# Eight weight tiles in a pool of their own at the upper end of SBUF

## The chip, the cores and the metric

The kernel runs on one core of one Trainium2 chip. The metric is the device time of one execution in microseconds (us); before the change the median of three runs is 2689.66 us, from 2688.57 to 2689.96. A core has TensorE (matmuls and transposes; PE in the profile, its loads of weights PEld), VectorE (DVE), ScalarE (ACT), GpSimd (POOL) and SyncE (SP), from whose queue this kernel issues its DMAs. SBUF is the memory on the core in which tiles lie; an address below is a byte offset in each of its 128 partitions. A matmul has a stationary operand, which a load of weights brings in, and a moving operand, which is read column by column.

## The reference

A trunk of two layers on 2048 rows of 1024 channels: a gated MLP with chunked spatial mixing, and band attention with a learned relative bias.

```python
# layer A
h = rms_norm(x, a_norm_g)
u, v, z = jnp.split(h @ w_in, 3, axis=-1)            # 1024 -> 3 x 2048
u = gelu(u); v = layer_norm(gelu(v), ln_g, ln_b)
mixed = einsum('hts,bgshc->bgthc', w_m, vg) + b_s    # 128-row chunks, masked
x = x + (u * mixed * silu(z)) @ w_out
# layer B
k, v = jnp.split(rms_norm(x, kv_norm_g) @ w_kv, 2, axis=-1)
q, z = jnp.split(rms_norm(x, b_norm_g) @ w_qz, 2, axis=-1)
sc = einsum('bqhd,bkhd->bhqk', q / 8, kc) + bias     # own and 8 earlier chunks of 64
o = einsum('bhqk,bkhd->bqhd', softmax(sc), vc)
x = x + (o * silu(z)) @ wb_out
return rms_norm(x, final_norm_g)
```

## The kernel before, in words

Each product in float32 is made as three matmuls in fp32r (`mm3`, lines 105 to 108): both operands are split into a high part, rounded by ScalarE, and a low part, which VectorE gets by subtracting the high part; the three matmuls add high times high, high times low and low times high. The lines 106, 107 and 108 of the profile are these three.

Layer A is done as block products in seven phases (`PH`, line 469) for each of six column groups of the input weights and for the output weights, after a scheme that needs seven products for eight blocks. A step is one phase of one pair of row blocks j: 12 matmuls for the input (`P` in the profile), 24 for the output (`Po`). The stationary operand is a tile of transposed activations, S, kept in DRAM and read again three steps ahead; the moving operand is T, the split combination of weight blocks that `make_t` (line 284) prepares: a DMA into a tile `raw` or `rw`, sums on GpSimd, then the high part by ScalarE (line 276) and the low part by VectorE (line 279). `in_t` (line 341) asks for the T tiles, two for each quarter of a phase, out of eight slots with the tag "T"; in the output projection the phases take turns between these slots and two large tiles, `hh` and `hl`, four quarters each (`in_big`, line 349).

Between the steps of layer A the gating stage runs: its mixing matmuls (`mx`, line 635) have the split mixing weights `ws` as stationary operand and the split normalized v, `vh` and `vl`, as moving operand; its results go to tiles `m`. These tiles lie in a pool `up` that is opened on the right side, from the upper end of SBUF downwards, and closed before the output projection. The pool `p0` of the first phases and the pool `po` of the output projection use the same end at other times.

Layer B normalizes and transposes 512 rows at a time (`norm_transpose`, line 128) into `hh` and `hl`, 16 KB per partition each. The projections (`one`, line 955, `pj` in the profile) have weights split by `load_split` (line 192) into two tiles of the tag "T" as stationary operand and `hh`, `hl` as moving operand; the projection of values (`vp`) has it the other way round; the output projection (`b4`, `bo`) moves weights of the tag "T" past the gated attention. Scores (`s`, line 1096), transposes of the probabilities (`tp`, line 1135) and their products with values (`pv`) are woven between the projections' matmuls by `take` (line 1314).

The pool `sh` (line 89) holds, from low to high addresses in the order of first use, four slots `raw` of 4 KB, the eight T slots of 4 KB, then `hh` and `hl`. Above it on the left side come the pools of layer A (`ca`, later `ug` and `poc`), and in layer B `cb` and `sb`.

Of the kernel before, what the change touches and what calls it, by code (L numbers as in the profile page):

```python
# [10 lines left out]
F32R = mybir.dt.float32r  # L11
# [6 lines left out]
P = 128  # L18
# [3 lines left out]
T = 512  # L22
# [11 lines left out]
def trunk_kernel(  # L34
# [52 lines left out]

    sm = ctx.enter_context(tc.tile_pool(name="sm", bufs=1))
    sh = ctx.enter_context(tc.tile_pool(name="sh", bufs=1))
    pmm = ctx.enter_context(tc.tile_pool(name="pmm", bufs=4, space=PSUM))  # L90

    class Late:
# [84 lines left out]
    def load_scaled(src, name, gain=None, keep=None):  # L177
        raw = sh.tile([P, 1024], F32, tag="raw", name=f"raw_{name}", bufs=4)
        nc.sync.dma_start(raw[:], src)
        if gain is not None:  # L180
            k = gain.shape[1]
            r3 = raw[:].rearrange("p (k c) -> p k c", k=k)
            nc.gpsimd.tensor_tensor(
                r3, r3, gain.broadcast_to([P, k, 1024 // k]), op=ALU.mult
            )
            if put_off:
                put_off[0](lambda: nc.sync.dma_start(keep, raw[:]))
            else:
                nc.sync.dma_start(keep, raw[:])
        return raw  # L190

    def load_split(*args):
        raw = load_scaled(*args)
        name = args[1]
        wh = sh.tile([P, 1024], F32R, tag="T", name=f"wh_{name}", bufs=8)
        wl = sh.tile([P, 1024], F32R, tag="T", name=f"wl_{name}", bufs=8)
        nc.scalar.copy(wh[:], raw[:])
        nc.vector.tensor_tensor(wl[:], raw[:], wh[:].bitcast(F32), op=ALU.subtract)
        return wh, wl
# [30 lines left out]
    with ExitStack() as actx:  # L230
# [110 lines left out]
        def in_t(n, ph):  # L341
            def where(q):
                return [
                    sh.tile([P, 1024], F32R, tag="T", name=f"T{n}_{ph}_{q}{i}", bufs=8)[:]
                    for i in range(2)
                ]
            return where
# [591 lines left out]
    with ExitStack() as bctx:  # L939
# [15 lines left out]
        def one(t, p, c):  # L955
            wh, wl = load_split(
                *kqz_source(t or p == 0, p, c)
            )
            acc = pmm.tile([P, T], F32, tag="mm", name=f"pj{t}_{p}_{c}")
            for k in range(KD):  # L960
                hh, hl = xT[t][k]
                sl = slice(k * P, (k + 1) * P)
                mm3(acc[:], wh[:, sl], wl[:, sl], hh, hl, k == 0, k == KD - 1)
                if k < KD - 1:
                    yield None
            yield acc

        def project(t, p, block=None):


            def proj_v(pp):
                w = []
                for half in range(2):
                    w.append(
                        load_split(
                            *v_source(t or pp == 0, pp, half)
                        )
                    )
# [216 lines left out]
        def b4(t, parts):  # L1195
# [5 lines left out]
            def prep(n):  # L1201
                if n == len(seq):
                    return
                dh, bl, k = seq[n]
                nm = f"{t}_{dh}_{bl[0]}_{k}"
                if k % 2 == 0:
                    wts[n] = wts[n + 1] = load_split(wb_out[dh, k // 2], f"bo{nm}")
                og = ogt[t, k]
                ts = slice(bl[0] * P, (bl[-1] + 1) * P)
                oh = sb.tile([P, len(bl) * P], F32R, tag="Q", name=f"oh{nm}", bufs=QB)  # L1210
                ol = sb.tile([P, len(bl) * P], F32R, tag="Q", name=f"ol{nm}", bufs=QB)
                nc.scalar.copy(oh[:], og[:, ts])
                nc.vector.tensor_tensor(ol[:], og[:, ts], oh[:].bitcast(F32), op=ALU.subtract)
                ogs[n] = (oh, ol)
# [210 lines left out]
```

## Time and profile before

| | before |
|---|---|
| median of 3 runs | 2689.66 us (2688.57 to 2689.96) |
| the profiled execution's own time | 2689.71 us |
| its span, first to last instruction | 2687.9 us |
| mean granted TensorE clock | 0.995 |
| bytes moved by DMA | 607.16 MB, 226 GB/s in the mean |

How to read it: the profile takes one execution. The span is the stretch from the first instruction to the last; the execution's own time has 1.8 us more around it. Groups of instructions are shown as line, engine, operation, written tile <- read tiles, shapes and count, then busy time in us and the mean of one in ns, then the idle time of the engine just before them and what ended it. Matmuls are pipelined: one lasts some 390 ns for 512 columns while the next starts 0.23 us after it. The view of one tile gives minimum, median and maximum instead of the mean.

The stages by time, from the profile's windows: TensorE is busy 288.65 of the first 300 us, 318.21 of the 320 us to 620, all of the 460 us to 1080, 269.84 of the 275 us to 1355 (the output projection of layer A and the end of what is before it), then 337.53 of 345, 647.40 of 650 and 323.95 of the last 338 us (attention).

### The profile page before, as it was taken

What the parts mean: (1) busy time and instruction counts of PE and PEld (TensorE: products, weight loads), DVE (VectorE), ACT (ScalarE), POOL (GpSimd) and SP (SyncE); (2) the same over time, 40 slices, a digit from 0 to 9 for tenths busy, and PEclk for the clock granted to TensorE, in tenths of its full rate; (3) what the DMA queues carried; (4) which work ended last, traced back from release to release, by engine and by line L of the source; (5) the groups of instructions that cost most, each with busy time, mean ns of one, the idle gap of its engine ahead of it and who ended that gap; (6) DMA issues with size and microseconds to landing.
All of it is one profiled execution on the core that took longest, in us unless ns stands there. A gap on an engine that the chain in (4) does not pass through costs nothing.

```text
span 2687.9 us, 39968 instructions
## 1 busy us (share of the span) xinstructions
PE 2645.6 (98%) x14176; PEld 2269.2 (84%) x14176; DVE 1933.5 (72%) x3187; ACT 1274.4 (47%) x2252; POOL 721.1 (27%) x775
## 2 busy tenths in 40 slices
PE   8999999999999999999999999999999999999997
PEld 7788888888888888788888888888988889888996
DVE  5655666766667667778666676877879777787777
ACT  5422242443434434323255554566655666556663
POOL 3511223141232413534034520211202111021110
PEclk9999999999999999999999999999999999999998
DMA  7899999986977868767576654544445454454331
GB/s 296 311 335 334 346 363 322 324 321 229 327 259 270 313 250 309 266 223 272 186 264 211 214 183 162 180 150 142 162 159 183 141 153 155 139 166 122 113 110 68
DMA packets 209190, 607.16 MB, mean 226 GB/s; under 512 B 24288, under 2 KB 24288, under 8 KB 208992
## 3 DMA queue, kind: packets, MB, share of 16 engines
q1 hardware_dynamic: 208992, 604.62, 65.4%
q8 instruction: 113, 1.85, 0.3%
q14 instruction: 85, 0.70, 0.1%
HBM read 466.11 MB, written 127.93 MB: 221 GB/s over the span
## 4 chain that ended last, share of the span: by engine, by line
PE 85%; DVE 5%; DMA 4%; POOL 2%; issue 2%; ACT 1%; SPq 0%; DVEq 0%; POOLq 0%; ACTq 0%
PE P L108 10%; PE P L107 10%; PE P L106 10%; PE pj L106 6%; PE pj L107 6%; PE pj L108 6%; PE s L1096 4%; PE tp L1135 4%; PE pv L1162 4%; PE Po L108 3%; PE Po L107 3%; PE Po L106 3%; PE vp L108 2%; PE vp L106 2%; PE vp L107 2%; PE bo L106 2%
## 5 line engine op out<-in xcount | busy, mean ns | idle before, releaser
L106 PE MATMUL P<-T,S 128*128 128x512 f32 x1248 | 495.1, 397 | 3.9 <-ACT S L276 2.1
L108 PE MATMUL P<-T,S 128*128 128x512 f32 x1248 | 489.4, 392 | 0.0
L107 PE MATMUL P<-T,S 128*128 128x512 f32 x1248 | 488.1, 391 | 1.1 <-DVE T L279 1.1
L1115 POOL TENSOR_SCALAR pr<-pr,sl 128x640 f32<-128x640 f32 (+4 forms) x256 | 202.0, 789 | 760.7 <-DVE sl L1114 662.2
L1111 ACT ACTIVATE pr<-pr,nm 128x640 f32<-128x640 f32 (+4 forms) x256 | 195.4, 763 | 266.2 <-DVE nm L1104 263.6
L106 PE MATMUL pj<-hh_b,wh_b 128*128 128x512 f32 x768 | 311.6, 406 | 0.2 <-ACT hh_b L166 0.2
L107 PE MATMUL pj<-hl_b,wh_b 128*128 128x512 f32 x768 | 302.6, 394 | 0.0
L108 PE MATMUL pj<-hh_b,wl_b 128*128 128x512 f32 x768 | 301.7, 393 | 0.0
L108 PEld LDWEIGHTS P<-T,S 128*128 128x128 f32 x1248 | 234.7, 188 | 50.1
L106 PEld LDWEIGHTS P<-T,S 128*128 128x128 f32 x1248 | 235.2, 188 | 49.4 <-ACT S L276 2.3
L107 PEld LDWEIGHTS P<-T,S 128*128 128x128 f32 x1248 | 235.2, 188 | 46.6 <-DVE T L279 1.3
L1139 DVE TENSOR_TENSOR pt<-tp,pt 128x640 fp32r<-128x640 f32 (+4 forms) x256 | 188.8, 738 | 59.7 <-ACT pt L1138 57.0
L1104 DVE CUSTOM_DVE_ANT_0 pr<-s,bias 128x640 f32<-128x640 f32 (+4 forms) x256 | 188.2, 735 | 46.7 <-PE s L1096 41.3
L108 PEld LDWEIGHTS pj<-hh_b,wl_b 128*128 128x128 f32 x768 | 144.4, 188 | 33.2
L1135 PE MATMUL tp<-ident,pr 128*128 128x128 f32 x1120 | 164.7, 273 | 6.2 <-DVE pt L1139 4.6
L1138 ACT CAST pt<-tp 128x640 fp32r<-128x640 f32 (+4 forms) x256 | 159.4, 623 | 22.6 <-PE tp L1135 18.0
L1135 PEld LDWEIGHTS tp<-ident,pr 128*128 128x128 f32 x1120 | 134.7, 140 | 33.6 <-POOL pt L1128 4.4
L106 PEld LDWEIGHTS pj<-hh_b,wh_b 128*128 128x128 f32 x768 | 144.8, 189 | 19.2 <-ACT hh_b L166 0.5
L107 PEld LDWEIGHTS pj<-hl_b,wh_b 128*128 128x128 f32 x768 | 145.2, 189 | 17.4
L106 PE MATMUL vp<-wh_bv,hh_b 128*128 128x256 f32 x512 | 148.5, 290 | 0.9 <-ACT hh_b L166 0.9
L108 PE MATMUL vp<-wh_bv,hl_b 128*128 128x256 f32 x512 | 145.6, 284 | 0.3
L107 PE MATMUL vp<-wl_bv,hh_b 128*128 128x256 f32 x512 | 145.2, 284 | 0.0
(220 smaller groups left out, 6052.4 us busy)
## 6 DMA issues: line engine op xcount, KB each, us to landing
S<-hsd SPq DMA_DIRECT2D x288, 512.0 KB, 5.0
rw<-in_w_a SPq DMA_DIRECT2D x108, 512.0 KB, 6.0
raw_b<-wk SPq DMA_DIRECT2D x75, 512.0 KB, 3.8
A<-ytd SPq DMA_DIRECT2D x72, 512.0 KB, 4.9
hsd<-S SPq DMA_DIRECT2D x56, 512.0 KB, 4.3
rwo<-in_w_out SPq DMA_DIRECT2D x40, 512.0 KB, 4.8
bias<-reld SPq DMA_DIRECT2D x64, 320.0 KB, 3.5
raw_bo<-in_wb_out SPq DMA_DIRECT2D x36, 512.0 KB, 3.9
```

The source lines that it names most:

```text
L106: mm(ps, lh, rh, start=first, stop=False)
L107: mm(ps, lh, rl, start=False, stop=False)
L108: mm(ps, ll, rh, start=False, stop=last)
L1096: mm(ps[:, sg, :w], q[:, qb * P : (qb + 1) * P], kx[:, koff + sg * w : koff + (sg + 1) * w], start=i == 0, stop=i == 1,)
L1104: nc.vector.tensor_tensor_reduce(out=pr[:, c0:].rearrange("p (a b) -> p a b", a=nseg), in0=ps[:, :nseg, :w], in1=bias[:, c0:].rearrange("p ...
L1111: nc.scalar.activation(pr[:, c0:], pr[:, c0:], AF.Exp, scale=-1.0, bias=nm[:], accum_out=sl[:])
L1115: nc.gpsimd.tensor_scalar(pr[:, c0:], pr[:, c0:], sl[:], 1.0, op0=ALU.mult, op1=ALU.mult)
L1135: tpose(tp[:, b, :], pr[:, b * P : (b + 1) * P], ident[:])
L1138: nc.scalar.copy(oh, tp[:, b0:5, :])
L1139: nc.vector.tensor_tensor(pt[:, 1, b0 + qq : 5 + qq, cs], tp[:, b0:5, :], oh.bitcast(F32), op=ALU.subtract)
L1162: mm(po[:, 0, :], keys(i), pt[:, j, i, :], start=(t == 0 and j == 0 and i == blocks[0]), stop=(j == 1 and i == blocks[-1]),)
```

## The change

The eight slots of the tag "T" move from the pool `sh` into a new pool `shT` that is opened right behind it with `side="right"`, so that it lies at the upper end of SBUF. Later pools on that side (`p0`, `up`, `po`) lie below it. The two tiles `hh` and `hl` of the transposed norm, which lay above T, take T's former place, and the left side's later pools start 32 KB lower.

```diff
@@ -87,6 +87,7 @@
     sm = ctx.enter_context(tc.tile_pool(name="sm", bufs=1))
     sh = ctx.enter_context(tc.tile_pool(name="sh", bufs=1))
+    shT = ctx.enter_context(tc.tile_pool(name="shT", bufs=1, side="right"))
     pmm = ctx.enter_context(tc.tile_pool(name="pmm", bufs=4, space=PSUM))
@@ -192,8 +193,8 @@
     def load_split(*args):
         raw = load_scaled(*args)
         name = args[1]
-        wh = sh.tile([P, 1024], F32R, tag="T", name=f"wh_{name}", bufs=8)
-        wl = sh.tile([P, 1024], F32R, tag="T", name=f"wl_{name}", bufs=8)
+        wh = shT.tile([P, 1024], F32R, tag="T", name=f"wh_{name}", bufs=8)
+        wl = shT.tile([P, 1024], F32R, tag="T", name=f"wl_{name}", bufs=8)
         nc.scalar.copy(wh[:], raw[:])
@@ -341,7 +342,7 @@
     def in_t(n, ph):
             def where(q):
                 return [
-                    sh.tile([P, 1024], F32R, tag="T", name=f"T{n}_{ph}_{q}{i}", bufs=8)[:]
+                    shT.tile([P, 1024], F32R, tag="T", name=f"T{n}_{ph}_{q}{i}", bufs=8)[:]
                     for i in range(2)
                 ]
             return where
```

The addresses in the two built programs, in bytes of a partition:

| tiles | before | after |
|---|---|---|
| `raw` (4 x 4096) | 4736 to 21120 | 4736 to 21120 |
| T (8 x 4096) | 21120 to 53888 | 196576 to 229344 |
| `hh`, `hl` (2 x 16384) | 53888 to 86656 | 21120 to 53888 |
| S (6 x 4096) | 137856 to 162432 | 105088 to 129664 |
| `ws` (2 x 4096) | 192480 to 200672 | 159712 to 167904 |
| `vh`, `vl` (3 x 4096) | 200672 to 212960 | 167904 to 180192 |
| `m` (4 x 4096) | 212960 to 229344 | 180192 to 196576 |

On no engine does an instruction change its place: the rows of the two programs stand in the same order on TensorE, VectorE, ScalarE, GpSimd and SyncE, with the same waits, so no rows are set against each other here. Below the new line 90 all line numbers are one higher.

## The prediction

> **What bounds the kernel now.** I read the page first: busy times, then the chain that ended last.
>
> ```profile
> span 2687.9 us, 39968 instructions
> ...
> PE 2645.6 (98%) x14176; PEld 2269.2 (84%) x14176; DVE 1933.5 (72%) x3187; ACT 1274.4 (47%) x2252; POOL 721.1 (27%) x775
> ...
> PE 85%; DVE 5%; DMA 4%; POOL 2%; issue 2%; ACT 1%; SPq 0%; DVEq 0%; POOLq 0%; ACTq 0%
> ```
>
> TensorE is busy for 2645.6 of 2687.9 us, so all that can be won or lost without touching its own pace is 42.3 us of idle time, and most of that is the start. So the time is 14176 matmuls times their pace, and a change matters here if it alters that pace or adds waits on TensorE. The execution profiled took 2689.71 us (span plus 1.8 us around it), 0.05 us over the median of 2689.66; the sum below is made against 2689.71. A measurement of this kernel tells about 0.2%, 5.4 us, from no change.
>
> Next, what TensorE waits for (microseconds in total, times, longest one):
>
> ```profile
> PE tp L1135 <- DVE pt L1139: 4.6, 3, 4.0
> ...
> PE P L107 <- DVE T L279: 1.1, 1, 1.1
> ...
> PE vp L106 <- ACT hh_b L166: 0.9, 3, 0.4
> ```
>
> The longest sum is 4.6 us. Waits for the writers of the tiles that the change moves are 1.1 us (T) and 0.9 us (hh): 2.0 us in the whole run. Their writers work far ahead.
>
> **The change part by part.** *Instructions.* None is added, removed or reordered: on all five engines the rows stand in the same order with the same waits, and each tile takes the same slot of its tag. What differs is addresses, in bytes of a partition. The eight T tiles go from 21120–53888 to 196576–229344. hh and hl go from 53888–86656 to 21120–53888, T's old place. Every other tile above them moves down by exactly 32768 and keeps its distance to its neighbours; raw stays. So the direct term is 0 instructions, 0 DMAs, 0 waits. What is left is whether an instruction takes longer or shorter because of where its operand lies.
>
> *T read by TensorE as the moving operand.* These are the dearest groups, with pj, where T is stationary and hh and hl move. Columns: count, busy us, mean ns.
>
> ```profile
> L106 PE MATMUL P<-T,S 128*128 128x512 f32 x1248 | 495.1, 397 | 3.9 <-ACT S L276 2.1 <-DMA S<-hsd 1.7
> L108 PE MATMUL P<-T,S 128*128 128x512 f32 x1248 | 489.4, 392 | 0.0
> L107 PE MATMUL P<-T,S 128*128 128x512 f32 x1248 | 488.1, 391 | 1.1 <-DVE T L279 1.1
> L106 PE MATMUL pj<-hh_b,wh_b 128*128 128x512 f32 x768 | 311.6, 406 | 0.2 <-ACT hh_b L166 0.2
> L107 PE MATMUL pj<-hl_b,wh_b 128*128 128x512 f32 x768 | 302.6, 394 | 0.0
> L108 PE MATMUL pj<-hh_b,wl_b 128*128 128x512 f32 x768 | 301.7, 393 | 0.0
> ...
> L106 PE MATMUL bo<-wh_bo,oh 128*128 128x512 f32 x256 | 101.2, 396 | 3.1 <-ACT oh L1212 3.1
> ...
> L106 PE MATMUL Po<-To,So 128*128 128x512 f32 x256 | 100.3, 392 | 0.0
> ```
>
> The means differ, 391 to 406 ns for the same shape, which could be the place of the operands. To see whether it is, take one stretch, 1120 to 1335 us, where the output projection reads its moving operand by turns from T and from hh and hl:
>
> ```profile
> L106 PE MATMUL Po<-To,So 128*128 128x512 f32 x166 | 64.6, 389 | 0.0
> L107 PE MATMUL Po<-To,So 128*128 128x512 f32 x166 | 64.6, 389 | 0.0
> ...
> L106 PE MATMUL Po<-To_hh,So 128*128 128x512 f32 x151 | 58.8, 389 | 0.0
> ...
> L107 PE MATMUL Po<-To_hl,So 128*128 128x512 f32 x151 | 58.7, 389 | 0.0
> ```
>
> 389 ns from all three regions. And the pj group itself, in a stretch where nothing of another shape stands between its matmuls (1358.5 to 1365.3 us), with the same hh, hl and T slots side by side:
>
> ```profile
> L107 PE MATMUL pj<-hl_b,wh_b 128*128 128x512 f32 x11 | 4.3, 390 | 0.0
> L108 PE MATMUL pj<-hh_b,wl_b 128*128 128x512 f32 x11 | 4.3, 390 | 0.0
> L106 PE MATMUL pj<-hh_b,wh_b 128*128 128x512 f32 x10 | 3.9, 389 | 0.0
> ```
>
> 389 to 390, not 406. The surplus therefore comes with the position in the stream (transposes and scores between the projection's matmuls), which is unchanged, and not with the place of hh, hl or T. hh and hl move into the very bytes that T is read from at 389 ns. Term: 0.
>
> *The upper end.* Before, the eight slots of 4 KB at 196576 to 229344 held exactly the second ws tile, the three vh and vl tiles and the four m tiles of the gating stage. TensorE read the first two kinds there, and ScalarE and VectorE wrote them. The gating matmuls mx answer for the reads (min/median/max ns), beside the nearest row at a low address, vp, which moves 256 columns of T (its mean follows its busy time):
>
> ```profile
> L106 PE MATMUL mx<-vh,ws x128: 280/282/283, 362.0 to 968.9; 128*128 128x256 f32 x128
> ```
>
> ```profile
> L107 PE MATMUL vp<-wl_bv,hh_b 128*128 128x256 f32 x512 | 145.2, 284 | 0.0
> ```
>
> 282 against 284 ns: nothing is lost at the upper end. It also answers for alignment: the slots of T started on a multiple of 64 bytes and now start 32 bytes past one, as vh, vl and ws did. Where T is the stationary operand, in pj, the load of weights is what reads it; loads from S and from the upper end (ws) stand against each other, in mean ns:
>
> ```profile
> L108 PEld LDWEIGHTS P<-T,S 128*128 128x128 f32 x1248 | 234.7, 188 | 50.1
> ...
> L108 PEld LDWEIGHTS mx<-vh,ws 128*128 128x128 f32 x128 | 24.1, 189 | 0.0
> ```
>
> What no row of before shows is a run of 512 moving columns that starts 32 bytes off. The bounds from the nearest rows: mx less vp, −2 ns, at the lower end; at the upper end pj's mean, (406 + 394 + 393) / 3 = 398, less 389, +9 ns. I take 0, since mx reads off that boundary twice in each matmul and shows no cost.
>
> *T written by ScalarE and VectorE.* Low address, then the same operations at the upper end:
>
> ```profile
> L276 ACT CAST T<-rw x42: 1028/1052/1085, 9.1 to 943.0; 128x1024 fp32r<-128x1024 f32 x42
> L279 DVE TENSOR_TENSOR T<-rw,T x42: 1209/1222/2311, 11.6 to 949.3; 128x1024 fp32r<-128x1024 f32 x42
> ```
>
> ```profile
> L276 ACT CAST vh<-va x32: 1036/1052/1057, 354.1 to 950.8; 128x1024 fp32r<-128x1024 f32 x32
> L279 DVE TENSOR_TENSOR vl<-va,vh x32: 1208/1225/2178, 355.2 to 959.7; 128x1024 fp32r<-128x1024 f32 x32
> ```
>
> Medians 1052 and 1052, 1222 and 1225: +3 ns on a subtraction. The loops make 258 such pairs (42 from rw as shown, 36 from the chain tiles, 16 for the output, 164 for the attention's weights), so 0.8 us of VectorE in 1933.5, behind TensorE's work. If that cover were gone, 0.8 us is the whole price. Term: 0.
>
> *Transfers.* No DMA writes T. Those into tiles that moved by 32768 are the same transfers to the same offsets; the commonest:
>
> ```profile
> S<-hsd SPq DMA_DIRECT2D x288, 512.0 KB, 5.0
> ```
>
> An S tile is asked for three steps ahead; a step is 12 matmuls, and the stretch of 215 us above has 950 of them, 0.226 us each, so 8.1 us ahead for a landing of 5.0. A change of 1 us in landing would stay hidden. Term: 0.
>
> Sum: 2689.71 + 0 = **2689.7 us**.
>
> **The rivals.** *Faster: parting the two operands of pj and the writers of T from its readers frees TensorE's reads.* Priced at the whole surplus over 389 ns: pj (17 + 5 + 4) × 768 = 20 us, P (8 + 3 + 2) × 1248 = 16 us; together 36 us, so 2654. Any part above 5.4 us would be seen. For it speaks only that the surplus exists. Against it speak the two quiet stretches, where neighbours read at 389. The Trainium skill, SBUF — State Buffer, section Who interferes with whom, says of engines at work together that "only the shared port pair causes contention", a pair of VectorE and GpSimd, and that TensorE and ScalarE wait on nobody. By that rule the parting gives 0 and the time stays 2689.7, where this rival's price would make it 2654. The trace agrees so far: TensorE holds 389 ns from 1120 to 1335 us while both other engines write its operands.
>
> *Slower: T's start off the 64-byte boundary costs each 512-column read.* T is the moving operand of 3744 matmuls in P, 768 in Po and 768 in bo (three times the counts of 1248, 256 and 256 above), 5280. At +9 ns each that is 48 us, so 2737. From 1 ns each, 5.3 us, it begins to show. mx speaks against it, but mx reads runs of 128 columns, not of 512; so it keeps a chance. The Trainium skill, same page, section Operand start alignment, has no price for such a start: it says that its runs there "timed nothing".
>
> *The same, by another way:* VectorE's subtractions reach 2311 ns beside GpSimd's work, and if those collisions shift by a microsecond, TensorE could wait a few times more or less. By the waits above, 2.0 us hang on such writers; 2687.7 to 2691.7 covers losing or doubling them. It counts as no change.
>
> **How the numbers follow.** No change, 2689.7: 0.86. Faster rival: 0.06. Slower rival: 0.08. These are the three chances for faster by over 0.2%, within it, and slower. The range: the likeliest case's own, with the doubled waits and the bound of 1 ns on 5280 reads below its edge, 2685.0 to 2694.5; the 14 in 100 left to the rivals may stay outside.
>
> **What would show it.** Right: P<-T,S again at 397, 392 and 391 ns, pj at 406, 394 and 393, each within 1; TensorE busy within 3 us of 2645.6; casts and subtractions at medians of 1052 and about 1225. Wrong to the faster side: pj's means fall towards 390 in the stretches with transposes between. Wrong to the slower side: Po<-To at 390 or more in a quiet stretch while Po<-To_hh stays at 389. If the sum of waits grows by over 5 us with the paces unchanged, it was collisions of the writers, which I count as nothing.

## The result, and the profile after

| | before | after |
|---|---|---|
| median | 2689.81 us (4 runs) | 2713.55 us (4 runs, 2713.19 to 2716.22) |
| ratio, 95% interval | 1 | 1.0093, 1.0081 to 1.0105 |
| span of the profiled execution | 2687.9 us | 2711.4 us |

The changed kernel is slower by 0.9%, 24 us, with the same instructions in the same order. First the page of after, the line of busy times:

```profile
span 2711.4 us, 39968 instructions
...
PE 2674.7 (99%) x14176; PEld 2268.6 (84%) x14176; DVE 1933.7 (71%) x3187; ACT 1273.9 (47%) x2252; POOL 721.3 (27%) x775
```

VectorE, ScalarE, GpSimd and the loads of weights are busy as long as before, within 0.6 us. TensorE's matmuls are busy 29 us longer and its idle time is shorter. So no wait was added; the matmuls themselves became longer. Which ones, by the groups of after (line numbers are one higher; busy us, mean ns):

```profile
L107 PE MATMUL P<-T,S 128*128 128x512 f32 x1248 | 500.7, 401 | 2.3 <-ACT S L277 2.1
L108 PE MATMUL P<-T,S 128*128 128x512 f32 x1248 | 495.5, 397 | 1.1 <-DVE T L280 1.1
L109 PE MATMUL P<-T,S 128*128 128x512 f32 x1248 | 493.2, 395 | 0.0
L107 PE MATMUL pj<-hh_b,wh_b 128*128 128x512 f32 x768 | 312.1, 407 | 0.2 <-ACT hh_b L167 0.2
L108 PE MATMUL pj<-hl_b,wh_b 128*128 128x512 f32 x768 | 304.2, 396 | 0.0
L109 PE MATMUL pj<-hh_b,wl_b 128*128 128x512 f32 x768 | 303.4, 395 | 0.0
...
L109 PE MATMUL Po<-To,So 128*128 128x512 f32 x256 | 101.7, 397 | 0.0
L107 PE MATMUL Po<-To,So 128*128 128x512 f32 x256 | 101.2, 395 | 0.0
...
L107 PE MATMUL bo<-wh_bo,oh 128*128 128x512 f32 x256 | 102.0, 398 | 3.1 <-ACT oh L1213 3.1
...
L107 PE MATMUL mx<-vh,ws 128*128 128x256 f32 x128 | 36.1, 282 | 0.0
```

P is at 401, 397 and 395 ns instead of 397, 391 and 392: 13 ns over its three lines, times 1248, is 16 us. Po from T has gone from 392, 389 and 389 to 395, 395 and 397, 17 × 256 = 4 us, and bo from 396, 394 and 395 to 398, 399 and 399, 11 × 256 = 3 us. pj is 1 to 2 ns a line longer, 5 × 768 = 4 us. Together that is 27 us; vp, 1 ns shorter on each of 1536 matmuls, gives 2 back. mx is where it was. And the quiet output projection, now 1128 to 1350 us, where the reads of T and of hh, hl take turns:

```profile
L109 PE MATMUL Po<-To,So 128*128 128x512 f32 x162 | 64.6, 399 | 0.0
L107 PE MATMUL Po<-To,So 128*128 128x512 f32 x163 | 63.9, 392 | 0.0
L108 PE MATMUL Po<-To,So 128*128 128x512 f32 x162 | 63.9, 394 | 0.0
L109 PE MATMUL Po<-To_hh,So 128*128 128x512 f32 x157 | 61.2, 390 | 2.0 <-DVE So L280 2.0
L107 PE MATMUL Po<-To_hh,So 128*128 128x512 f32 x156 | 60.7, 389 | 0.0
```

Before, all were at 389. Now the matmuls that move T take 392 to 399 and those that move hh stay at 389 to 390. That is the sign named for the slower rival. Writers of T did not change: casts of T from rw have a median of 1048 ns and subtractions of 1222, against 1052 and 1222 before:

```profile
L277 ACT CAST T<-rw x42: 1032/1048/1082, 9.3 to 957.4; 128x1024 fp32r<-128x1024 f32 x42
L280 DVE TENSOR_TENSOR T<-rw,T x42: 1211/1222/2308, 11.7 to 963.9; 128x1024 fp32r<-128x1024 f32 x42
```

### The profile page after: what moved, and what is told of

It reads as the page before. It is cut to its first block, busy times and chain, and to the rows that moved or that the text cites. A ratio compares the mean times of both kernels' runs of the same rounds, so it can differ in the third digit from the quotient of the medians.

```text
span 2711.4 us, 39968 instructions
## 1 busy us (share of the span) xinstructions
PE 2674.7 (99%) x14176; PEld 2268.6 (84%) x14176; DVE 1933.7 (71%) x3187; ACT 1273.9 (47%) x2252; POOL 721.3 (27%) x775
## 5 line engine op out<-in xcount | busy, mean ns | idle before, releaser
L107 PE MATMUL P<-T,S 128*128 128x512 f32 x1248 | 500.7, 401 | 2.3 <-ACT S L277 2.1
L108 PE MATMUL P<-T,S 128*128 128x512 f32 x1248 | 495.5, 397 | 1.1 <-DVE T L280 1.1
L109 PE MATMUL P<-T,S 128*128 128x512 f32 x1248 | 493.2, 395 | 0.0
```

Source lines behind the costliest of these rows:

```text
L107: mm(ps, lh, rh, start=first, stop=False)
L108: mm(ps, lh, rl, start=False, stop=False)
L109: mm(ps, ll, rh, start=False, stop=last)
```

## The experiments

Three theories. A: T's slots now start off a boundary of 64 bytes, and each operand pays for its own start. B: the place costs, the upper end or the new distances. C, formed after the first four runs: what counts is the difference between the starts of the moving and the stationary operand.

**T at the upper end, 32 bytes lower** (against the changed kernel).

```diff
+    shp = ctx.enter_context(tc.tile_pool(name="shp", bufs=1, side="right"))
+    shp.tile([P, 8], F32, name="padt")
     shT = ctx.enter_context(tc.tile_pool(name="shT", bufs=1, side="right"))
```

> The changed kernel with one unused tile of 32 bytes above T: the eight T slots stay at the upper end, but start at 196544, a multiple of 64 bytes, as they did at 21120; the other pools on the right side come 32 bytes lower too. Theory A (the start of T's slots 32 bytes off a 64-byte boundary makes each 512-column read of T longer): 2690 us, within 3, Po<-To and P<-T,S back at means of 389 to 397 ns. Theory B (the upper end of SBUF, or the new distances between T, hh, hl and S, make reads longer): 2713 us, within 3, Po<-To at 395 to 397 ns.

Measured: 2698.74 us against 2687.98, ratio 1.0042 (1.0028 to 1.0057). Neither theory: about half of the loss is gone. T is on a multiple of 64 and still 11 us too slow. The groups of this run:

```profile
L109 PE MATMUL P<-T,S 128*128 128x512 f32 x1248 | 499.0, 400 | 3.1 <-ACT S L279 2.0 <-DVE T L282 0.9
...
L109 PE MATMUL pj<-hh_b,wh_b 128*128 128x512 f32 x768 | 314.0, 409 | 0.2 <-ACT hh_b L169 0.2
...
L110 PE MATMUL vp<-wl_bv,hh_b 128*128 128x256 f32 x512 | 143.3, 280 | 0.0
...
L109 PE MATMUL bo<-wh_bo,oh 128*128 128x512 f32 x256 | 102.1, 399 | 3.1 <-ACT oh L1215 3.1
```

By all lines of each group, P is 6 us longer than before, pj 6, bo 4 and Po from T 2, and vp is 5 us shorter.

**T in its old place, 32 bytes higher**, and **hh and hl alone 32 bytes off**. Both give T and hh, hl pools of their own on the left side, with an unused tile of 32 bytes ahead of one and another behind it:

```diff
     sh = ctx.enter_context(tc.tile_pool(name="sh", bufs=1))
+    shp = ctx.enter_context(tc.tile_pool(name="shp", bufs=1))
+    shp.tile([P, 8], F32, name="padt")
+    shT = ctx.enter_context(tc.tile_pool(name="shT", bufs=1))
+    shq = ctx.enter_context(tc.tile_pool(name="shq", bufs=1))
+    shq.tile([P, 8], F32, name="padq")
+    shH = ctx.enter_context(tc.tile_pool(name="shH", bufs=1))
```

(this is the first; the second has `shT` ahead of `padt`, and `padq` behind `shH`; the lines that ask for T in `shT` and for hh and hl in `shH` are left out)

> The kernel before, T in its old place between raw and hh, but 32 bytes higher (21152), and hh, hl and all above by 64 bytes, so that only T leaves its 64-byte boundary. Theory A: 2713 us, within 4, Po<-To and P<-T,S 4 to 6 ns longer in the mean, Po<-To_hh unchanged at 389. Theory B: 2690 us, within 3, nothing longer.

> The kernel before, T in its old place, only hh and hl 32 bytes off a 64-byte boundary. Theory A: the 576 matmuls of the output projection that read hh and hl get 6 to 7 ns longer (4 us), those of layer A's first group (288) add 1 to 2 us, and pj's 2304, whose moving operand they are, 2 to 7 ns each (5 to 15 us): 2699 to 2711 us. Theory B: 2690 us, within 3.

Measured: 2710.36 us, 1.0085 (1.0070 to 1.0100), for T; 2716.63 us, 1.0108 (1.0093 to 1.0123), for hh and hl. So the loss comes without any move to the upper end, and B, as it was stated, falls. The second outcome is above what A gave, and its profile says why:

```profile
L112 PE MATMUL P<-T,S 128*128 128x512 f32 x1248 | 502.3, 403 | 2.2 <-ACT S L282 1.9 <-DMA S<-hsd 0.2
...
L112 PE MATMUL Po<-To_hh,So 128*128 128x512 f32 x192 | 76.1, 396 | 0.6 <-ACT So L282 0.6
```

The reads of hh went from 390 to 396, as A had it. But P, which reads T at its old address, went from 397 to 403 as well. The unused tiles had raised the S tiles by 64 bytes there, and S is P's stationary operand. A cannot say why P pays when S moves from one multiple of 64 to another.

**Series of matmuls alone**, which take the disputed cost by itself. `mo` and `so` are the starts of the moving and the stationary operand in elements of 4 bytes, within two tiles, the second 32768 bytes behind the first:

```python
def series(name, mo, so, n, k=1, gap=0, count=60):
    ...
    for i in range(count):
        lo = (i % 4) * 1024 + mo
        ...
        st = (i % 4) * 512 + so
        nc.tensor.matmul(ps[i % 4][:, :n], sta[:, st : st + P], rhs, start=True, stop=True)
```

> No layer is computed, x is copied to the output; beside it TensorE runs series of 60 matmuls of fp32r alone, each with a load of weights, that differ only in where the operands start: moving operand of 512 columns at 0, 4, 8, 16, 32, 48, 64 and 96 bytes past a 64-byte boundary, stationary operand at 16, 32 and 64, both at 32, 256 columns at 0 and 32, and four runs of 128 columns at 0 and 32. Theory A: about 227 ns from start to start at 0 and 64, about 233 at every other start of the moving operand, and no more at 48 than at 4; at 256 columns no difference, if the load of weights hides it. Theory B: all series of 512 columns alike within 1 ns.

Four of the series, in the view of one tile (min/median/max ns, first and last start):

```profile
L76 PE MATMUL mzero<-mov,sta x60: 388/389/390, 37.5 to 50.8; 128*128 128x512 f32 x60
L76 PE MATMUL mthirtytwo<-mov,sta x60: 393/396/397, 93.2 to 106.9; 128*128 128x512 f32 x60
L76 PE MATMUL sthirtytwo<-mov,sta x60: 392/396/397, 162.9 to 176.6; 128*128 128x512 f32 x60
L76 PE MATMUL both<-mov,sta x60: 388/389/397, 190.9 to 204.3; 128*128 128x512 f32 x60
```

The moving operand 32 bytes on costs 7 ns; the stationary operand 32 bytes on costs the same; both together cost nothing. A falls: an operand's own start is not what counts. At 256 columns a start 32 bytes on costs nothing (117.8 ns from start to start against 120.0), so a row of 256 columns could not have shown it. The shape of the read matters too: with the 512 columns in four runs of 128, 64 bytes apart, alike starts took 240.0 ns and the moving operand 32 bytes on 231.7.

**All of the left side raised by 96 bytes**, so that hh, hl, S and Q start as far past a multiple of 128 as T does at the upper end.

```diff
-    cst.tile([P, 40], F32, name="pad")
+    cst.tile([P, 64], F32, name="pad")
```

> The changed kernel with the unused tile of the constants 96 bytes larger: T stays at the upper end at 196576, which is 96 past a multiple of 128; raw, hh, hl, S, Q, K, V, the probabilities and all else on the left side move up by 96 bytes, so that they start 96 past a multiple of 128 as well. Only the identity stays at 0. Theory A (each operand pays for its own start off a boundary): more than 2713 us, since hh, hl, S and Q leave the boundary too; 2715 to 2735. Theory C (what counts is the difference between the start of the moving operand and that of the stationary one, within 128 bytes; alike is fast): 2690 us, within 4, with Po<-To and Po<-To_hh back at 389 ns; the transposes, whose operands now differ, may add up to 2 us.

Measured: 2692.59 us against 2689.62, 1.0011 (1.0002 to 1.0021). T has not moved by a byte from the changed kernel, and the loss is gone but for some 3 us (see the open ends below). The groups of this run:

```profile
L107 PE MATMUL P<-T,S 128*128 128x512 f32 x1248 | 495.9, 397 | 3.7 <-ACT S L277 2.1 <-DMA S<-hsd 1.6
L109 PE MATMUL P<-T,S 128*128 128x512 f32 x1248 | 488.6, 391 | 0.0
...
L108 PE MATMUL Po<-To,So 128*128 128x512 f32 x256 | 99.7, 389 | 0.0
```

P and Po are back at 397, 391 and 389. The transposes, which were thought to add something, did not: 273 ns in both.

**Many pairs of starts**, the same series.

> No layer is computed, x is copied to the output; TensorE alone runs series of 60 matmuls of fp32r, each with a load of weights, over many pairs of starts (moving, stationary), in steps of 32 bytes, for 512, 256 and 320 columns, and then blocks of five 128-column matmuls and six of 512 columns for ten pairs. Theory C: at 512 columns 226.7 ns from start to start at every pair with the same remainder of 128, (64,64), (96,96), (128,0), (0,128) and (256,0) among them, and 229 to 237 at the others; the price is the same for (32,0) and (96,64). Theory A: 226.7 only where both are multiples of 64 or 128. In the blocks, which imitate the projections, theory C expects the pair of equal starts to be no slower than any other; if one of the unequal pairs is faster there, a layout other than both kernels' may pay for the projections.

```profile
L76 PE MATMUL xf_ea<-mov,sta x60: 388/392/398, 65.1 to 78.6; 128*128 128x512 f32 x60
L76 PE MATMUL xf_ia<-mov,sta x60: 392/394/398, 92.8 to 106.6; 128*128 128x512 f32 x60
L76 PE MATMUL xf_qa<-mov,sta x60: 389/389/397, 148.9 to 162.3; 128*128 128x512 f32 x60
L76 PE MATMUL xf_ae<-mov,sta x60: 393/396/398, 245.8 to 259.6; 128*128 128x512 f32 x60
L76 PE MATMUL xf_am<-mov,sta x60: 388/392/398, 301.8 to 315.3; 128*128 128x512 f32 x60
L76 PE MATMUL xf_gg<-mov,sta x60: 387/389/398, 412.1 to 425.5; 128*128 128x512 f32 x60
```

(moving, stationary) in bytes, downwards: (64,0), (128,0), (256,0), (0,64), (0,192), (96,96). (128,0) is slow, against what C expected, and (256,0) is fast: the period is 256 bytes, not 128. (64,0) and (0,192), the same difference modulo 256, share 392; (0,64) does not. From the starts in the trace, the mean from start to start over the last 47 of each 60, by the difference, moving less stationary, modulo 256:

| difference | 512 columns, ns | pairs |
|---|---|---|
| 0 | 226.7 | (0,0), (256,0), (0,256), (64,64), (96,96) |
| 64 | 228.8 | (64,0), (320,0), (0,192), (128,64) |
| 32, 96 | 233.3 | (32,0), (96,0), (96,64), (64,32) |
| 128 | 232.2 to 233.4 | (128,0), (0,128), (384,0) |
| 160 | 234.2 to 234.4 | (160,0), (0,96) |
| 192, 224 | 233.3 to 233.4 | (192,0), (0,64), (224,0), (0,32) |

It accounts for most of what the kernels did. Within 256 bytes, T, hh, hl, S and Q all start at 128 before. After, T is at 224, so P has a difference of 96. With 32 bytes above it, T is at 192: a difference of 64 for P, the cheap one, and of 192 for pj, where T is stationary, a dear one. With hh and hl off by 32, S is at 192 and T at 128, a difference of 192. The kernels can be read in the same measure as the series, from start to start, if each unbroken run of matmuls of one group is counted from its seventh on (pauses over 300 ns left out):

| run | P, ns (series) | pj, ns (series) |
|---|---|---|
| before | 227.5 (226.7) | 228.1 (226.7) |
| after | 233.4 (233.3) | 234.5 (234.2) |
| T 32 bytes lower | 228.9 (228.8) | 233.4 (233.3) |
| left side raised by 96 | 227.4 (226.7) | 228.7 (226.7) |

pj comes mostly in runs of six between other matmuls, and only 145 of its 2304 stand in longer ones; that fits the small loss in its rows above. One group does not fit: with T 32 bytes lower, bo has P's difference of 64 and yet took 232.5 ns.

For 256 columns the same series have another best case: 120.0 ns at 0, 113.3 at 192:

```profile
L76 PE MATMUL xt_aa<-mov,sta x60: 280/283/287, 495.4 to 502.5; 128*128 128x256 f32 x60
...
L76 PE MATMUL xt_ma<-mov,sta x60: 276/276/286, 538.0 to 544.8; 128*128 128x256 f32 x60
```

In the blocks that imitate the projections, (0,0) was the fastest of the ten pairs, 1933 ns a block against 1943 to 1967; it tied with none, not even with (32,32) at 1943, although those starts are alike. So none of the ten pairs promises a gain for pj.

**The last 256-column reads put where their series are fastest**, one group at a time and both.

```diff
+                if t == 0 and h == 0 and g == 0:
+                    sb.tile([P, 48], F32, tag="pd", name="pd", bufs=1)
                 pt = sb.tile([P, 2, 6, 256], F32R, tag="PT", name=f"pt{t}_{h}_{g}", bufs=2)
+                if t == 0 and h == 0 and g == 0:
+                    sb.tile([P, 16], F32, tag="pe", name="pe", bufs=1)
```

> The kernel before with the transposed probabilities alone, the moving operand of pv, 192 bytes past the start (within 256) that everything else on the left side has. The series gave 113.3 ns from start to start for 256 columns at a difference of 192 and 120.0 at 0. Theory C, with 256 for its period: pv's 960 matmuls of line 1162 gain up to 6 ns each, 5.8 us: 2684 us, within 2. If the waits and shapes between them set their pace: no change, 2690 within 2. Theory A: no gain.

```diff
-        wh = sh.tile([P, 1024], F32R, tag="T", name=f"wh_{name}", bufs=8)
+        o = 48 if name.startswith("bv") else 0
+        wh = tpool[0].tile([P, 1088], F32R, tag="T", name=f"wh_{name}", bufs=8)[:, o : o + 1024]
```

(`wl` likewise; left out are the two pools that take the T slots, one for layer A and one, `tpool[0]`, for layer B)

> The kernel before with the eight T slots in two pools, for layer A at 53888 and for layer B in slots of 4352 bytes at the same place, hh and hl at 21120; all starts stay alike within 256 bytes, but the value projection's weights, its moving operand, start 192 bytes into their slots. Theory C: vp's 1536 matmuls gain up to 6.6 ns each, 10 us: 2680 us, within 4; pj unchanged. A gain under 3 us says that vp's pace in the kernel is not that of the series.

> Both shifts of 192 bytes together. Theory C: 2674 us, within 5, the sum of both gains, and faster than either kernel of this case. Otherwise whatever the two give.

Measured against 2689.80: the transposed probabilities 2686.62, 0.9986 (0.9978 to 0.9995); the value projection 2685.11, 0.9982 (0.9973 to 0.9991); both 2680.65, 0.9968 (0.9956 to 0.9980). Each is a gain, about half of what the series promised and short of the forecast (2684, 2680 and 2674 us). Both together are 9 us faster than the kernel before, no less than the sum of the two gains, 3 and 5 us. The run with both:

```profile
L106 PE MATMUL vp<-wh_bv,hh_b 128*128 128x256 f32 x512 | 145.8, 285 | 0.9 <-ACT hh_b L166 0.9
L108 PE MATMUL vp<-wh_bv,hl_b 128*128 128x256 f32 x512 | 142.6, 279 | 0.4
L107 PE MATMUL vp<-wl_bv,hh_b 128*128 128x256 f32 x512 | 142.4, 278 | 0.0
L1170 PE MATMUL pv<-pt,V 128*128 128x256 f32 x576 | 103.6, 284 | 0.0
```

vp's lines are at 285, 278 and 279 against 290, 284 and 284 before, 16 ns × 512 = 8 us; pv gains 3 ns on its first group, not 6. From the seventh of a run on it gains more, from 119.2 ns from start to start to 113.8; but its runs are mostly of ten, between scores, transposes and projections. In the run of the value projection alone a wait of 1.9 us for the rearranged weights takes part of it back:

```profile
L106 PE MATMUL pj<-hh_b,wh_b 128*128 128x512 f32 x768 | 312.1, 406 | 1.9 <-ACT wh_b L199 1.9
```

**Finer starts**, and transposes.

> No layer is computed, x is copied to the output; series of 60 matmuls as before: 512 columns at differences of 16 to 240 in odd multiples of 16, 256 columns at every multiple of 16 and with the stationary operand moved instead, 128 columns at multiples of 32, and transposes against an identity at multiples of 32. Theory C: at 512 columns nothing under 226.7; at 256 columns 113.3 at 192, and a moved stationary operand at 64 gives the same as a moving one at 192; transposes within 3 ns of each other.

At 512 columns nothing came under 226.7 ns, but a difference of 240 gave 226.7 too, which the multiples of 32 had not shown; the other odd multiples of 16 gave 231.1 to 234.6. The stationary operand moved by 16 is the same difference as 240, and the first series had 233.3 for it: in steps of 16 the difference is not the whole law. At 256 columns 112 and 192 both gave 113.3. The stationary operand moved by 64, the same difference as 192, gave 117.8, and moved by 192 it gave 113.3 here but 117.8 in the run of many pairs. So at 256 columns the law is not the difference alone, and something else enters that these runs do not name. Series of 128 columns stayed at 111.7 ns and transposes at 109.2, whatever the start.

**The changed kernel with 96 bytes above T**, which brings T to 196480, 128 within 256.

```diff
+    shp.tile([P, 24], F32, name="padt")
     shT = ctx.enter_context(tc.tile_pool(name="shT", bufs=1, side="right"))
```

> The changed kernel with an unused tile of 96 bytes above T, in place of none or of 32 bytes: T at the upper end at 196480, which leaves 128 within 256 bytes, as hh, hl, S and Q do. Theory C with the period of 256: the whole loss is gone, 2690 us, within 4, P<-T,S at 397, 392 and 391 ns and Po<-To at 392, 389 and 389. Theory A (a boundary of 64 or 128 bytes of T alone) gives the same here, and is told apart by the run with all at 96 and the one with hh and hl off. Theory B (the upper end itself costs): 2698 or more.

Measured: 2688.53 us against 2688.59, 0.9998 (0.9990 to 1.0007). The whole loss is gone with T still at the upper end:

```profile
L109 PE MATMUL P<-T,S 128*128 128x512 f32 x1248 | 497.8, 399 | 3.3 <-ACT S L279 2.0 <-DMA S<-hsd 1.1
L110 PE MATMUL P<-T,S 128*128 128x512 f32 x1248 | 489.3, 392 | 0.6 <-DVE T L282 0.6
...
L111 PE MATMUL bo<-wh_bo,ol 128*128 128x512 f32 x256 | 100.6, 394 | 0.7 <-DVE ol L1216 0.7
```

## Why the prediction was wrong, step by step

The forecast was 2689.7 us with a range from 2685.0 to 2694.5; the time was 2713.55, outside, on the side of the slower rival, which had 0.08.

- **What bounds the kernel** was right. TensorE's pace sets the time, and the whole change is in it; waits on the moved tiles stayed at 1.1 us for T.
- **Instructions, writers, transfers: 0** was right. The rows kept their order, VectorE and ScalarE their durations, and DMAs into S landed after 4.8 us in place of 5.0.
- **The upper end: 0** was the step that failed, in its second half. The place is innocent, as the run with 96 bytes above T shows. What counted was T's start against that of its partner: with T at 224 and S at 128 within 256 bytes, P's lines took 3 to 6 ns more, 16 of the 24 us. But the text let mx answer for alignment too, "since mx reads off that boundary twice in each matmul and shows no cost". Two things can have hidden the cost there, and no run tells which. Its operands vh, vl and ws were all displaced alike, 224 within 256 bytes, so that their difference was 0. And mx moves 256 columns, in two runs of 128, and the series of 256 unbroken columns show no cost of a displaced start; none had the shape of mx. The row nearest in place was not near in what mattered.
- **The quiet stretch at 389 ns from all three regions** was read rightly but proved less than it was made to: T, hh, hl and S all started at 128 within 256, so it could say nothing of unlike starts.
- **The faster rival** fell: parting T from hh and from the other tiles won nothing. With alike starts at the upper end the ratio is 0.9998. The rule of the Trainium skill, SBUF — State Buffer, section Who interferes with whom, that engines do not hold TensorE up agrees with this. Its table calls TensorE's two read ports, for the moving operand and for loads of weights, independent; here the measurement does not fit it, since 226.7 ns become 233.4 when the stationary operand alone starts 32 bytes on. Whether the ports are the reason was not shown.
- **The slower rival** had the sign, the place (T as moving operand, P, Po and bo) and the sign by which to know it. Its mechanism, T's own start, was wrong, and its price of 9 ns came from pj's surplus, which is another thing: measured were 2 to 8 ns a line, 16 us for P, 4 for Po and 3 for bo, so 23 us in place of 48. pj, where T is stationary, was not in its price and gave 4 us. That its sign came true was in part luck: with the left side raised by 96 bytes T starts just as far off a boundary, and the time is 2692.59.
- **The range.** The text counts the bound of 1 ns on 5280 reads as inside it; 2689.7 + 5.3 is 2695.0, just above its edge of 2694.5. Nothing hangs on that.

What stays open is why the difference of two starts matters, and why 64 is cheap and 192 is not. In the series a load of weights lasts 188 ns and begins some 3 ns after the matmul before it, so the moving operand of one matmul and the weights of the next are read side by side; in every series of one pair, and in P, all weights start alike within 256 bytes, so no run tells whether a matmul's own weights count or the next one's. All series ran on zeros, and differences finer than 16 bytes were tried only at 4 and 8 (236.6 and 233.3 ns).

Of the residue of 3 us with the whole left side raised, its profile shows some 2 us: Po's reads of hh and hl are at means of 392 to 393 ns in place of 389 to 390, because a few of them, from 1107 to 1111 us and behind a wait for So, last up to 628 ns. The granted clock was 0.72 from 1105 to 1111 us, against 1.00 in the same stretch before. Whether other executions had this is not known.

## What to carry to other kernels

A change of addresses alone can move a kernel bound by TensorE: compare the starts of moving and stationary operands modulo 256 bytes before and after, and keep those of 512-column fp32r matmuls alike, with a tile of padding if a pool ends elsewhere. When a row of the trace is to answer for a new case, ask in which respect it is alike; a pair of operands displaced together says nothing of one displaced alone. A series of sixty matmuls, with one start changed at a time, tests such a question in a single run.

## What the runs showed of the hardware that was not expected

With each matmul bringing its own weights, the pace of 512 fp32r columns in a quiet stream is 226.7 ns or between 229 and 237 ns. In the series in steps of 32 bytes the difference of the two starts modulo 256 bytes decides it to within 1.2 ns; alike starts reached 226.7 ns wherever they were tried, though (32,32) and (96,96) did so only after some eight matmuls. At 256 columns alike starts are among the slowest, 120.0 ns, and a moving operand 112 or 192 bytes on is the fastest seen, 113.3; 192, used for the value projection and the probabilities, made the kernel 0.3% faster than before, 2680.65 us. At 320 columns the seven pairs tried all gave 146.7 ns.
